# Linear attention's gate computed with its weights moving, its decay levels in three visits instead of four, and two changes of who issues DMAs

## The chip, the cores and the metric

The kernel runs on one core of a Trainium2 chip. TensorE (PE in the profile) multiplies, VectorE (DVE) and ScalarE (ACT) prepare operands and finish results, GpSimd (POOL) does little here, and SyncE (SP) issues nearly all DMAs. The metric is device time in microseconds of one launch, as the median of several runs.

## The reference, cut to what matters

Two layers on x (256 x 2048, fp32). Each layer projects x, runs three groups of heads, gates each with a SiLU path, projects back and normalizes:

```python
h = x @ w_in                                  # 2048 -> 6672 columns
a_q, a_k, a_v, a_z, b_q, b_k, b_v, b_z, b_lr, m_q, m_z = jnp.split(h, cuts, axis=-1)
y_a = chunk_band_attention(heads_a(a_q), heads_a(a_k), heads_a(a_v), rel_table)   # 8 heads of 128
log_g = log_sigmoid(b_lr @ gate_w + gate_b) / 16
o_b = gla_chunk_recurrence(b_q, b_k, b_v, log_g)     # linear attention, 4 heads, chunks of 64
y_b = o_b * rsqrt(mean(o_b**2) + 1e-6) * gla_norm_g
mk, mv = jnp.split(mem @ w_mem_kv, 2, axis=-1)
y_m = memory_attention(m_q, mk, mv)                  # 4 heads of 128
y = concat([y_a * silu(a_z), y_b * silu(b_z), y_m * silu(m_z)])
x = layer_norm(ALPHA * x + y @ w_out, ln_g, ln_b)
```

Within a chunk of 64 frames the linear attention (GLA) weighs frame j for frame i by exp(-|b_i - b_j|), where b is the running sum of the log gates, with one decay per key dimension.

## The kernel before

**Precision.** Every fp32 operand of the large products is split into a high part (`wh`, or `x[..., 0]`), rounded to the fp32r type, and a low part (`wl`, or `x[..., 1]`), which is the rest. A product is high times high, high times low and low times high. ScalarE casts the high part (line 261), VectorE subtracts to get the low part (line 268), each one or two loads ahead of TensorE.

**Two forms of a product.** Line numbers are those of the profile; every product is issued by the helper `mm` (line 86). In `stationary`, a 128x128 tile of the weights is loaded into the array and the activations move: for each 128 of the inner dimension two matmuls of 512 columns (high and low activations side by side, both against `wh`) and two of 256 (against `wl`). The result lies with features on the partitions. `ws_pieces` calls it for a group of 512 output features in two halves of four loads each, four units to a load, and hands each half to a `put` function. In `moving` the activations are loaded into the array and the weights move: three matmuls of 512 columns for each 128 tokens. The result lies with tokens on the partitions. `as_pieces` calls it for 512 features in eight loads, four units to a load. A load of either form is 512 KB, and a unit of either form streams 1536 columns: two matmuls of 512 and two of 256 in the one, three of 512 in the other.

**What sets the order.** TensorE and SyncE run in the order in which the program is written; the order of the other engines comes from a scheduler. `loads` is one list of all weight loads in the order of use. `take` hands out the next load and, ahead of it, issues later casts, subtractions and DMAs; a raw load goes to a ring of four buffers (`RAWS`), so a DMA on SP waits until the subtraction four loads back is done. The work of the heads is written as generators. `tick` is called once after each load (or each quarter product) and lets the generators whose time has come issue their next piece; `yield 3` means: go on three ticks later. A generator in `aside` (GLA, residual, norms) runs beside the heads in `waiting`, two heads at a time. `banks(n)` gives n of four PSUM banks, and yields until they are free. `finish` ticks until the named generators are done.

**GLA.** After the sums of the log gates, the attention inside a chunk is computed in levels (`LEVELS` 32 to 1, and -1 for the diagonal). For each level `distance` and `decayed` make decayed keys and queries on VectorE and ScalarE, each in a 128x512 buffer of the pool `sc` (eight buffers); TensorE then does 16 products of 64x64 (32 matmul records, since plain fp32 goes in two passes), and VectorE copies the part that belongs to the level into `pairs`. A turn of this on TensorE is a visit; there are four, of two, two, two and one levels, with two PSUM banks each (three in the last, which also makes the chunk states). After the visits come the products with the values and states, a norm (line 698) and four transposes per head parity (line 704), which write `yraw[0]` with features on the partitions.

**The gates.** Six groups follow the values: the second keys of the banded attention, the memory queries, then the gates b_z, a_z (two groups) and m_z, all as `ws_pieces`. `gate` adds the two halves of a result (`total`: line 497 on ScalarE, line 498 on VectorE), applies SiLU, waits with `finish` for its heads, multiplies `yraw` (line 1119) and, for b_z, splits it at once (`split_y`).

**Output stage and end.** The output projection works with seven products of blocks instead of eight (`out_unit`, letters B, K and T of the strings `OUT_B`, `OUT_A`; O is a plain `as_pieces`), so B and T loads are used for six matmuls and K and O loads for twelve. In the last layer `gain_rows` fetches the rows of ln_g and ln_b, broadcast to 128 partitions, as eight DMAs of 256 KB on POOL's queue, all in one place; `norm_residual` does the same for the layer before on SP's queue.

**Start.** `begin` issues on SP a quarter of the first activations (128 KB), the first weights (512 KB), the rest of these activations, and the second weights.

Of the kernel before, what the change touches and what calls it, by code (L numbers as in the profile page):

```python
# [16 lines left out]
P = 128  # L17
# [10 lines left out]
VISITS = ((-1, 0), (1, 2), (3, 4), (5,))  # L28
# [24 lines left out]
def hybrid_trunk_kernel(  # L53
# [71 lines left out]

    def banks(n):
        while len(free) < n:
            yield 1
        return [free.pop(0) for _ in range(n)]
# [11 lines left out]
    def plan():  # L141
        for l in range(L):
            def keys(p):
                g = w512[l, G_MK].rearrange("(h q) p n -> q p h n", h=2)
                return Load(g[p // 2, :, :, p % 2 * 512:p % 2 * 512 + 512], (2, 512))
# [46 lines left out]
            for g in (G_AK1, G_MQ, G_BZ, G_AZ0, G_AZ1, G_MZ):  # L192
                loads.extend(Load(w512[l, g, p], (4, 256)) for p in range(8))
# [143 lines left out]
    def begin():  # L337

        x, ws = loads[0], loads[1:3]
        xt = operand()  # L340
        x.quarter[0].append(xt)
        x.hi, x.lo = xt[:, :, 0], xt[:, :, 1]
        x.raw = res.rearrange("p t (s j n) -> p (t s) j n", s=2, j=4)[:, 0]
        for w in ws:
            w.raw = wp.tile([P, 2, 512], F32, name=nm("raw"), tag="raw")
            w.hi = wp.tile([P, 2, 512], F32R, name=nm("wh"), tag="wh", bufs=4)
            w.lo = wp.tile([P, 2, 512], F32R, name=nm("wl"), tag="wl", bufs=3)
        zero = zeros(dve, 256)
        whole = slice(None)
        first, second = slice(0, 256), slice(256, 512)  # L350
        for d, s in ((x, (whole, 0)), (ws[0], (whole,)), (x, (whole, slice(1, 4))), (ws[1], (whole,))):
            src = d.src if d is x else d.src.rearrange("p (k n) -> p k n", k=2)
            sp.dma_start(d.raw[s], src[s])
        parts = [(x, (whole, 0)), (ws[0], (whole, 0, first)), (ws[0], (whole, 0, second)), (ws[0], (whole, 1)), (x, (whole, 1)),
                 (x, (whole, 2)), (ws[1], (whole, 0)), (x, (whole, 3)), (ws[1], (whole, 1))]
        at["dma"] = 3
        for i in range(ZEROS):
            mm(ps[:, 2 + i % 2, :256], zero[:, :P], zero, True, True)
        for d, s in parts:
            cast = act.copy(d.hi[s], d.raw[s])  # L360
# [172 lines left out]
    def gla(gb, ng, gq, gk, asv, yraw):  # L533
# [38 lines left out]
        def distance(lev):  # L572
            s = LEVELS[lev]
            bm = b_.rearrange("p (g c) -> p g c", c=2 * s)
            dd = scratch([P, 512])
# [6 lines left out]
        def decayed(dd):  # L582
            kl = scratch([P, 512])
# [12 lines left out]
        yield 3  # L596

        kdT = yraw[:, 0:2].rearrange("p h (g c) -> p (h g) c", c=P)
        st = hd.tile([P, 3, 2, P], F32, name=nm("st"), tag="st")
        for v, levels in enumerate(VISITS):  # L600
# [8 lines left out]
            pb = yield from banks(3 if last else 2)  # L609
            for i, (lev, (kl, ql)) in enumerate(zip(levels, ready)):  # L610
                o = 256 if last else i * 256
                for t in range(2):
                    for b in range(2):
                        for half in range(2):
                            for par in range(2):
                                rs = slice(par * 64, par * 64 + 64)
                                c0 = b * T + t * P + half * CH
                                mm(ps[half * CH:(half + 1) * CH, pb[par], o + (t * 2 + b) * CH:o + (t * 2 + b + 1) * CH],
                                   kl[rs, c0:c0 + CH], ql[rs, c0:c0 + CH], True, True)
# [11 lines left out]
            for i, lev in enumerate(levels):  # L631
                o = 256 if last else i * 256
                for par in range(2):
                    pv = ps[:, pb[par], o:o + 256].rearrange("p (g c) -> p g c", c=CH)
# [30 lines left out]
        place = lambda par, half: slice((par ^ half) * CH, (par ^ half) * CH + CH)  # L665
        for g in range(4):
            t, b = g // 2, g % 2
            for par in range(2):
                for half in range(2):
                    hs = slice(half * CH, (half + 1) * CH)  # L670
                    mm(ps[place(par, half), bx[half], g * P:(g + 1) * P], pairs[par][hs, g],
                       asv[hs, t, 16 + (2 * b + par) * P:16 + (2 * b + par + 1) * P], True, True)
        for odd, even in ((1, 2), (3, None)):
            for b in range(2):
                for c in (odd, even):
                    if c is not None:
                        for par in range(2):
                            rs = slice(par * 64, par * 64 + 64)
                            g = (c // 2) * 2 + b
                            mm(ps[place(par, c % 2), by[par], g * P:(g + 1) * P],  # L680
                               qe[rs, b * T + c * CH:b * T + (c + 1) * CH], st[rs, c - 1, b], True, True)
        for half in range(2):
            for par in range(2):
                hs = place(par, half)
                act.copy(on[par][hs], ps[hs, bx[half]].rearrange("p (g c) -> p g c", c=P))
# [13 lines left out]
        yield 4  # L699
        for par in range(2):  # L700
# [4 lines left out]
            y = yraw.rearrange("p (b e) (t h c) -> p e h b t c", e=2, t=2, h=2)[:, par]  # L705
            o = ps[:, pt].rearrange("p (b t h c) -> p h b t c", b=2, t=2, h=2)
            for half in range(2):
                act.activation(y[:, half], o[:, half ^ par], AF.Copy, scale=ng[:, 0:1])
# [265 lines left out]
    for l in range(L):  # L974
# [102 lines left out]
        gens = [[gla(*gp, gq, gk, asv, yraw[0])]]  # L1077
# [35 lines left out]
        for i in range(4):  # L1113
            def gate(j, a, b):
                sz = gated()
                total(sz, a, b)
                act.activation(sz, sz, AF.Silu)  # L1117
                finish(gens[i])
                dve.tensor_tensor(yraw[i][:, j:j + 2], sz, yraw[i][:, j:j + 2], op=ALU.mult)  # L1119
                if i == 0:  # L1120
                    split_y(0, j)
                elif i == 3 and j == 2:
# [11 lines left out]
        if last:  # L1134
            rows = gain_rows(l)
# [133 lines left out]
```

## Time and profile before

| | |
|---|---|
| median of 3 runs | 913.99 us (912.38 to 914.93) |
| profiled execution, its own time | 913.39 us |
| its span, first to last instruction | 911.4 us (2.0 us lie around it) |
| granted TensorE clock | 0.999 |
| TensorE busy | 903.2 us of 911.4 |
| VectorE, ScalarE, GpSimd busy | 717.9, 551.8, 13.6 us |
| read from HBM | 193.16 MB |

A matmul's record is longer than the distance to the next one, because matmuls overlap; for the cost of a product the distance between starts is to be read, not the mean duration. In the timeline, a row merges neighbours of one kind (xcount), and an idle time in front is given in brackets with what ended it. In the windows, `DMA share` is the busy share of the 16 DMA engines.

### The profile page before, as it was taken

How to read it: one execution, taken by the hardware profiler on the slowest of the kernel's cores; microseconds unless marked ns; L12 is line 12 of the kernel's file. 1: busy time of each engine (PE TensorE's matmuls, PEld its weight loads, DVE VectorE, ACT ScalarE, POOL GpSimd, SP SyncE). 2: the span in 40 equal slices, each digit the busy share in tenths (PEclk: the TensorE clock that was granted, in tenths of full speed). 3: DMA queues.
4: the chain of work that ended last, by engine and by line, in shares of the span. 5: the costliest groups of instructions: out<-in, count | busy, mean ns of one | idle time of the engine just before them, and what ended most of it. 6: DMA issues, size and time to landing. Idle time of an engine off the chain costs nothing.

```text
span 911.4 us, 14553 instructions
## 1 busy us (share of the span) xinstructions
PE 903.2 (99%) x5491; PEld 795.3 (87%) x5491; DVE 717.9 (79%) x995; ACT 551.8 (61%) x809; POOL 13.6 (1%) x32
## 2 busy tenths in 40 slices
PE   9999999999999999999999999999999999999997
PEld 7889989998888888888888899999988888888885
DVE  5697688698766777799979767886886778778996
ACT  5675655576576675555559655556756667566540
POOL 1000000000000000000000000000000000100000
PEclk9999999999999999999999999999999999999999
DMA  8868786775445446876775787666754565776652
GB/s 298 293 195 288 262 266 206 236 253 180 160 145 161 159 161 187 289 272 223 236 243 167 206 291 254 223 196 186 218 177 134 178 192 185 273 277 232 229 190 93
DMA packets 64294, 196.21 MB, mean 215 GB/s; under 512 B 7008, under 2 KB 9568, under 8 KB 64224
## 3 DMA queue, kind: packets, MB, share of 16 engines
q1 hardware_dynamic: 63200, 193.08, 64.9%
q0 software_dynamic: 1024, 2.21, 0.8%
q8 instruction: 43, 0.70, 0.3%
q14 instruction: 27, 0.22, 0.1%
HBM read 193.16 MB, written 2.10 MB: 214 GB/s over the span
## 4 chain that ended last, share of the span: by engine, by line
PE 98%; DVE 1%; DMA 0%; ACT 0%; issue 0%; SPq 0%; DVEq 0%
PE ps L86 96%; PE ps L737 1%; DVE wl L268 0%; DMA raw<-w 0%; PE ps L833 0%; PE ps L775 0%; PE ps L704 0%; DVE sz L498 0%; DVE x L268 0%; ACT wh L261 0%; PE ps L606 0%; ACT res L877 0%; PE ps L541 0%; DVE term L260 0%; ACT wh L360 0%
## 5 line engine op out<-in xcount | busy, mean ns | idle before, releaser
L268 DVE TENSOR_TENSOR wl<-raw,wh 128x1024 fp32r<-128x1024 f32 (+1 forms) x313 | 364.8, 1169 | 118.5 <-PE ps L86 71.1
L261 ACT CAST wh<-raw 128x1024 fp32r<-128x1024 f32 (+1 forms) x313 | 313.9, 1008 | 233.4 <-PE ps L86 125.3
L86 PE MATMUL ps<-x,wh 128*128 128x512 f32 x1408 | 445.0, 397 | 0.0
L86 PEld LDWEIGHTS ps<-x,wl 128*128 128x128 f32 x1408 | 264.2, 188 | 63.2 <-DVE wl L268 1.0
L86 PE MATMUL ps<-x,wl 128*128 128x256 f32 x1408 | 277.5, 279 | 0.3 <-DVE wl L268 0.3
L86 PE MATMUL ps<-wh,x 128*128 128x512 f32 (+2 forms) x856 | 246.5, 369 | 0.9 <-ACT wh L360 0.9
L86 PEld LDWEIGHTS ps<-x,wh 128*128 128x128 f32 x1408 | 219.2, 189 | 1.6 <-issue 0.3
L86 PEld LDWEIGHTS ps<-wh,x 128*128 128x128 f32 x856 | 155.5, 188 | 19.7 <-ACT wh L360 1.1
L86 PE MATMUL ps<-wl,x 128*128 128x512 f32 (+2 forms) x428 | 157.8, 369 | 0.1
L86 PEld LDWEIGHTS ps<-wl,x 128*128 128x128 f32 x428 | 80.3, 188 | 10.5 <-DVE wl L268 0.6
L261 ACT CAST wh<-term 128x776 fp32r<-128x776 f32 (+1 forms) x39 | 36.0, 924 | 51.2 <-DVE term L260 43.3
L268 DVE TENSOR_TENSOR wl<-term,wh 128x776 fp32r<-128x776 f32 (+1 forms) x39 | 41.5, 1065 | 12.7 <-PE ps L86 12.0
L260 DVE TENSOR_TENSOR term<-term,term 128x776 f32<-128x776 f32 (+1 forms) x39 | 41.3, 1060 | 0.2 <-DMA term<-w 0.2
L86 PE MATMUL ps<-wh,s 128*128 128x512 f32 (+1 forms) x144 | 41.2, 367 | 0.0
L86 PEld LDWEIGHTS ps<-wh,s 128*128 128x128 f32 x144 | 25.8, 188 | 3.1
L86 PE MATMUL ps<-wl,s 128*128 128x512 f32 (+1 forms) x72 | 26.6, 370 | 0.3 <-DVE wl L268 0.3
L498 DVE SCALAR_TENSOR_TENSOR sz<-ps,sz 128x512 f32<-128x512 f32 x24 | 16.4, 687 | 5.0 <-ACT sz L497 4.1
L728 ACT ACTIVATE sc<-sc,mx 128x128 f32<-128x128 f32 (+1 forms) x32 | 14.2, 444 | 8.2 <-DVE mx L726 8.2
L86 PE MATMUL ps<-wh,sc 128*128 128x388 f32 x64 | 16.5, 338 | 0.0
L86 PEld LDWEIGHTS ps<-wl,s 128*128 128x128 f32 x72 | 13.5, 188 | 2.3 <-DVE wl L268 0.8
L1119 DVE TENSOR_TENSOR yr<-sz,yr 128x512 f32<-128x512 f32 x16 | 11.0, 687 | 4.6 <-ACT sz L1117 4.6
L1117 ACT ACTIVATE sz<-sz 128x512 f32<-128x512 f32 x16 | 10.1, 632 | 7.1 <-DVE sz L498 7.0
(222 smaller groups left out, 713.9 us busy)
## 6 DMA issues: line engine op xcount, KB each, us to landing
raw<-w SPq DMA_DIRECT2D x254, 512.0 KB, 4.3
raw<-w SPq DMA_DIRECT2D x64, 388.0 KB, 3.8
term<-w SPq DMA_DIRECT2D x24, 388.0 KB, 4.3
term<-w SPq DMA_DIRECT2D x15, 512.0 KB, 5.3
bias<-relw SPq DMA_DIRECT2D x16, 192.0 KB, 3.9
res<-xT SPq DMA_DIRECT2D x4, 512.0 KB, 6.9
res<-xn SPq DMA_DIRECT2D x4, 512.0 KB, 5.4
raw<-memT SPq DMA_DIRECT2D x4, 512.0 KB, 4.5
```

The source lines that it names most:

```text
L86: pe.matmul(o, l, r, start=start, stop=stop, skip_group_check=True)
L260: in_order(dve.tensor_tensor(d.raw, d.raw, d.plus, op=ALU.add))
L261: act.copy(d.hi, d.raw)
L268: in_order(dve.tensor_tensor(d.lo, d.raw, d.hi.bitcast(F32), op=ALU.subtract))
L498: dve.scalar_tensor_tensor(dst, a, scale, dst, op0=ALU.mult, op1=ALU.add)
L728: act.activation(s[:, own[t]], s[:, own[t]], AF.Exp, bias=mx[:, t:t + 1], accum_out=zs[:, t:t + 1])
L737: pe.transpose(ps[:, pt, i * P:(i + 1) * P], s[:, i * P:(i + 1) * P], ident)
L1117: act.activation(sz, sz, AF.Silu)
L1119: dve.tensor_tensor(yraw[i][:, j:j + 2], sz, yraw[i][:, j:j + 2], op=ALU.mult)
```

## The change

- `G_BZ`'s loads are cut as the memory keys' are (two runs of 512 instead of four of 256), and the group runs as `as_pieces` with its weights moving. Its `put`, `put_gate`, applies SiLU to the 128x1024 result straight from PSUM and hands it to GLA. `gla` multiplies its output (tokens on the partitions) by the gate before the four transposes, instead of `gate` doing it after them; the halves need no adding. `split_y(0, ...)` moves to the first half of the next gate.
- `VISITS` is three long, of three, three and one levels; the first two take four banks. A request for more than one bank now holds back requests for one (`wanted`). The third level's decayed keys and queries of the second visit go to `yraw[3]`.
- The copies after GLA's value products put each half of a chunk's rows in its place, so the last copy to `yraw[0]` is one per parity instead of two.
- `gain_rows` becomes a generator that issues one of its eight DMAs every two ticks, on SP's queue.
- The first quarter of the first activations is issued by ScalarE instead of SP.

```diff
-VISITS = ((-1, 0), (1, 2), (3, 4), (5,))
+VISITS = ((-1, 0, 1), (2, 3, 4), (5,))
...
     def banks(n):
-        while len(free) < n:
+        if n > 1:
+            wanted.append(n)
+        while len(free) < n or wanted and n == 1:
             yield 1
+        if n > 1:
+            wanted.remove(n)
         return [free.pop(0) for _ in range(n)]
...
             for g in (G_AK1, G_MQ, G_BZ, G_AZ0, G_AZ1, G_MZ):
-                loads.extend(Load(w512[l, g, p], (4, 256)) for p in range(8))
+                loads.extend(keys(p, g) if g == G_BZ else Load(w512[l, g, p], (4, 256)) for p in range(8))
...
-            sp.dma_start(d.raw[s], src[s])
+            (act if s == (whole, 0) else sp).dma_start(d.raw[s], src[s])
...
         ready = [(gkf, gqf), decayed(dd)]
         yield 3
+        ready.append(decayed(distance(1)))
+        yield 4
...
-            pb = yield from banks(3 if last else 2)
+            pb = yield from banks(3 if last else 4)
...
-                for lev in VISITS[v + 1]:
-                    dd = distance(lev)
+                for n, lev in enumerate(VISITS[v + 1]):
+                    mine, other = (extra[:, h * 2:h * 2 + 2].rearrange("p h t -> p (h t)") if n == 2 else None for h in range(2))
+                    dd = distance(lev, mine)
                     yield 1
-                    ready.append(decayed(dd))
+                    ready.append(decayed(dd, other))
                     yield 1
-                yield 1
+                yield 3
...
             dve.tensor_tensor(on[par], on[par], rr[:, par * 4:par * 4 + 4].unsqueeze(2).to_broadcast([P, 4, P]), op=ALU.mult)
-        yield 4
+        gate.append(None)
+        while len(gate) < 2:
+            yield 1
+        z = gate[1].rearrange("p t (b e d) -> p e (t b) d", e=2, d=P)
+        for par in range(2):
+            dve.tensor_tensor(on[par], on[par], z[:, par], op=ALU.mult)
+        yield 2
...
-    def gain_rows(l):
-        rows = []
+    def gain_rows(l, rows):
         for n in range(4):
-            g, b = scratch([P, 512]), scratch([P, 512])
-            pool.dma_start(g, ln_g[l:l + 1, columns(n)].to_broadcast([P, 512]))
-            pool.dma_start(b, ln_b[l:l + 1, columns(n)].to_broadcast([P, 512]))
-            rows.append((g, b))
-        return rows
+            pair_ = []
+            for a in (ln_g, ln_b):
+                pair_.append(scratch([P, 512]))
+                sp.dma_start(pair_[-1], a[l:l + 1, columns(n)].to_broadcast([P, 512]))
+                if a is ln_b:
+                    rows.append(pair_)
+                yield 2
...
+        def put_gate(acc):
+            while not z_gate:
+                tick()
+            z = hd.tile([P, 2, 512], F32, name=nm("z"), tag="qb")
+            act.activation(z, acc, AF.Silu)
+            z_gate.append(z)
+
+        run(as_pieces(xq[l], 512, put_gate, True))
+        for i in range(1, 4):
             def gate(j, a, b):
...
+                if i == 1 and j == 0:
+                    finish(gens[0])
+                    split_y(0, 0)
+                    split_y(0, 2)
                 finish(gens[i])
                 dve.tensor_tensor(yraw[i][:, j:j + 2], sz, yraw[i][:, j:j + 2], op=ALU.mult)
-                if i == 0:
-                    split_y(0, j)
```

How the order of instructions changes, at three places. In the rows, a buffer's number stands behind its name; `sc` are buffers of the pool of eight, `x` the four quarters of the activations, `qk` heads' queries and keys, `asv` the values.

First, TensorE in layer 0, at GLA's first visit, which before lay among the value loads (388 columns):

```order
L86 MATMUL ps<-wh_1870,x_474 128x388 x2
L86 MATMUL ps<-wl_1917,x_474 128x388
L606 MATMUL ps<-ident,sc_1819 128x128 x4
L86 MATMUL ps<-gq_506,gk_507 64x64 x16
L86 MATMUL ps<-sc_1824,sc_1888 64x64 x16
L86 MATMUL ps<-wh_1915,x_526 128x388 x2
L86 MATMUL ps<-wl_1942,x_526 128x388
```

and after the change:

```order
L86 MATMUL ps<-wh_1983,x_565 128x388 x2
L86 MATMUL ps<-wl_2013,x_565 128x388
L617 MATMUL ps<-ident,sc_1819 128x128 x4
L86 MATMUL ps<-gq_506,gk_507 64x64 x16
L86 MATMUL ps<-sc_1824,sc_1888 64x64 x16
L86 MATMUL ps<-sc_1976,sc_1980 64x64 x16
L86 MATMUL ps<-x_434,wh_2011 128x512 x2
L86 MATMUL ps<-x_434,wl_2031 128x256 x2
```

The first visit now has three levels and stands some loads later, between the last value load and the first load of the second keys.

Second, TensorE in layer 0 at GLA's transposes. Before, they stand beside products of a banded head in the memory queries' group, a load ahead of the gate's:

```order
L704 MATMUL ps<-ident,sc_2546 128x128 x4
L704 MATMUL ps<-ident,sc_2547 128x128 x4
L86 MATMUL ps<-sc_2685,asv_522 128x256
L86 MATMUL ps<-sc_2685,asv_522 128x128
L86 MATMUL ps<-sc_2690,asv_522 128x256
L86 MATMUL ps<-sc_2690,asv_522 128x128
L86 MATMUL ps<-x_565,wh_2660 128x512 x2
L86 MATMUL ps<-x_565,wl_2694 128x256 x2
```

and after the change:

```order
L86 MATMUL ps<-x_474,wh_2911 128x512 x2
L86 MATMUL ps<-x_474,wl_2937 128x256 x2
L721 MATMUL ps<-ident,sc_2675 128x128 x4
L721 MATMUL ps<-ident,sc_2676 128x128 x4
L86 MATMUL ps<-x_526,wh_2935 128x512 x2
L86 MATMUL ps<-x_526,wl_2959 128x256 x2
```

The transposes now stand behind the gate's eight loads, two loads (32 matmuls) and one memory head's first products into the next group. On ScalarE, the gate's SiLU (`z`) stands among the weight casts like this:

```order
L268 CAST wh_2935<-raw_2869 128x1024
L761 COPY yr_1679<-ps 128x256 x2
L268 CAST wh_2957<-raw_2897 128x1024
L1134 ACT_TABLE_LOAD
L1134 ACTIVATE z_2953<-ps 128x1024
L268 CAST wh_3005<-raw_2915 128x1024
L780 ACT_TABLE_LOAD
```

The cast behind `z` waits with it for the last matmul of the gate.

Third, SyncE in layer 1's output stage, before (`term` and `raw` are buffers of weights):

```order
L231 DMA term_8001<-w 128x1024
L238 DMA raw_8057<-w 128x1024
L238 DMA raw_8106<-w 128x1024
L238 DMA raw_8118<-w 128x1024
L238 DMA raw_8131<-w 128x1024
L238 DMA raw_8149<-w 128x1024
L238 DMA raw_8161<-w 128x1024
```

and after the change:

```order
L238 DMA term_7917<-w 128x1024
L245 DMA raw_7973<-w 128x1024
L245 DMA raw_8006<-w 128x1024
L821 DMA sc_8014<-ln_g 128x512
L245 DMA raw_8020<-w 128x1024
L245 DMA raw_8033<-w 128x1024
L821 DMA sc_8047<-ln_b 128x512
L245 DMA raw_8053<-w 128x1024
L245 DMA raw_8065<-w 128x1024
L821 DMA sc_8079<-ln_g 128x512
```

One row DMA now stands ahead of every second weight DMA, eight times in all.

More of the change, by code (lines that the diff above doesn't have):

```diff
@@ L531, in gla_inputs, with gla @@
         return gb, ng
-    def gla(gb, ng, gq, gk, asv, yraw):
+    def gla(gb, ng, gq, gk, asv, yraw, gate, extra):
         gqf = gq.rearrange("p b t -> p (b t)")
@@ L570, in gla, with distance @@
         act.activation(eb, b_, AF.Exp, scale=1.0 / 16)
-        def distance(lev):
+        def distance(lev, dd=None):
             s = LEVELS[lev]
             bm = b_.rearrange("p (g c) -> p g c", c=2 * s)
-            dd = scratch([P, 512])
+            if dd is None:
+                dd = scratch([P, 512])
             dve.tensor_tensor(dd.rearrange("p (g c) -> p g c", c=2 * s), bm,
@@ L664, in gla @@
         by = bx[2:]
-        place = lambda par, half: slice((par ^ half) * CH, (par ^ half) * CH + CH)
+        rows = lambda half: slice(half * CH, (half + 1) * CH)
         for g in range(4):
@@ L669, in gla @@
                 for half in range(2):
-                    hs = slice(half * CH, (half + 1) * CH)
-                    mm(ps[place(par, half), bx[half], g * P:(g + 1) * P], pairs[par][hs, g],
+                    hs = rows(half)
+                    mm(ps[rows(par ^ half), bx[half], g * P:(g + 1) * P], pairs[par][hs, g],
                        asv[hs, t, 16 + (2 * b + par) * P:16 + (2 * b + par + 1) * P], True, True)
@@ L704, in gla @@
                     pe.transpose(ps[:, pt, b * T + t * P:b * T + (t + 1) * P], on[par][:, t * 2 + b], ident)
[L705 to L708, printed above, removed]
+            y = yraw.rearrange("p (b e) t -> p e b t", e=2)[:, par]
+            act.activation(y, ps[:, pt].rearrange("p (b t) -> p b t", b=2), AF.Copy, scale=ng[:, 0:1])
             release(pt)
@@ L1134, in hybrid_trunk_kernel @@
         if last:
-            rows = gain_rows(l)
+            rows = []
+            beside([gain_rows(l, rows)])
             gbrow = per.tile([2, 1024], F32, name="gbrow", tag="yr0")
```

33 lines of the change are left out of this document (17 added, 16 removed).

## The prediction

> **What bounds the kernel now.** I read the page first, then the chain, then TensorE's own waits.
>
> ```profile
> span 911.4 us, 14553 instructions
> PE 903.2 (99%) x5491; PEld 795.3 (87%) x5491; DVE 717.9 (79%) x995; ACT 551.8 (61%) x809; POOL 13.6 (1%) x32
> PE 98%; DVE 1%; DMA 0%; ACT 0%; issue 0%; SPq 0%; DVEq 0%
> ```
>
> TensorE is busy for 903.2 of 911.4 us, and the chain that ended last runs through it for 98%. So an instruction taken from VectorE or ScalarE is worth nothing by itself, and a DMA is worth something only where TensorE stands still for it. What is left: the distance between starts of matmuls, the few places where TensorE is held up, and the start. The holdups are short, and a busy engine hides them, since a matmul's record is longer than its distance to the next. In the timeline they are gaps between starts; the three largest behind the start:
>
> ```profile
> 58.41 0.63 PE L86 MATMUL ps<-x,wh 128*128 128x512 f32 x2
> 59.31 0.50 PE L86 MATMUL ps<-x,wl 128*128 128x256 f32 x2 [0.26 <-DVE wl L268]
> ...
> 379.72 0.63 PE L86 MATMUL ps<-wh,s 128*128 128x512 f32 x2
> 380.67 0.50 PE L86 MATMUL ps<-wl,s 128*128 128x512 f32 x1 [0.31 <-DVE wl L268]
> ...
> 395.36 0.61 PE L86 MATMUL ps<-wh,x 128*128 128x512 f32 x2
> 396.12 0.50 PE L86 MATMUL ps<-wl,x 128*128 128x512 f32 x1
> ```
>
> Two matmuls of 512 take about 0.46 us from start to start; here they take 0.90, 0.95 and 0.76. That is 0.44 + 0.49 + 0.30 = 1.2 us lost to late low parts, at a layer's first own products and in layer 0's output stage. The change reorders nothing there.
>
> **The change part by part.** *The gate with weights moving.* The first two rows are the first and last of 15 units in the b_z group of layer 0 (stationary form), then the next instruction; the last two span seven units of the moving form.
>
> ```profile
> 272.38 0.63 PE L86 MATMUL ps<-x,wh 128*128 128x512 f32 x2
> ...
> 282.60 0.39 PE L86 MATMUL ps<-x,wl 128*128 128x256 f32 x2
> 282.83 0.38 PE L737 MATMUL ps<-ident,sc 128*128 128x128 f32 x2
> ...
> 442.18 0.62 PE L86 MATMUL ps<-wh,x 128*128 128x512 f32 x2
> ...
> 446.94 0.39 PE L86 MATMUL ps<-wh,x 128*128 128x512 f32 x1
> ```
>
> Stationary: (282.83 - 272.38) / 15 = 0.697 us a unit. Moving: (446.94 - 442.18) / 7 = 0.680 us. Both stream 1536 columns; the difference of 0.017 us is what four matmuls cost more than three. The gate has 8 loads of 4 units, 32 in a layer and 64 in both: 64 x 0.017 = 1.09 us less, all on TensorE's path. I take the whole, since both forms run here without a wait.
>
> The Trainium skill speaks against this size: "TensorE: Matmul & The Clock Gate", section "Wait — 56ns, not 53.3ns?", has warm matmuls start N/2.4 GHz plus about 2.5 ns apart, so one matmul less in each of 64 units would be worth an estimated 0.16 us. By it the sum would be 0.9 us smaller. The trace does not agree: a third of 0.680 is 0.227 us for 512 columns, 11 ns more than by that rule.
>
> *Three visits instead of four.* Every level keeps its 32 small matmuls; what goes is one change from the large products to small ones and back. The price comes from the visit of two levels, and from the first visit, where the levels follow each other.
>
> ```profile
> 197.46 0.69 PE L86 MATMUL ps<-gq,gk 64*64 64x64 f32 x32
> 197.98 0.65 PE L86 MATMUL ps<-sc,sc 64*64 64x64 f32 x32
> 198.55 0.62 PE L86 MATMUL ps<-wh,x 128*128 128x388 f32 x2
> ...
> 228.40 0.63 PE L86 MATMUL ps<-x,wh 128*128 128x512 f32 x2
> 228.87 0.39 PE L86 MATMUL ps<-x,wl 128*128 128x256 f32 x2
> 229.19 1.16 PE L86 MATMUL ps<-sc,sc 64*64 64x64 f32 x64
> 230.28 0.73 PE L86 MATMUL ps<-x,wh 128*128 128x512 f32 x2
> 230.84 0.40 PE L86 MATMUL ps<-x,wl 128*128 128x256 f32 x2
> ```
>
> From 228.40 to 230.84 are 2.44 us; without the visit they would be two pairs of 512 (0.47 each) and one of 256 (0.23), 1.17 us, so the visit cost 1.27. A level inside costs at least 0.45 and at most 0.52 (197.46 to 197.98, which holds some of the way in). Two levels are 0.90 to 1.04, and the change back and forth 0.23 to 0.37. I take 0.30 a layer, 0.6 us in all (bounds 0.46 to 0.74). That the first visit moves behind the value loads changes nothing, since it is inserted in the same way there.
>
> What could be late instead: the three levels wait for four banks, and heads that want one wait too. A head that waits costs nothing as long as its gate does not come first. In the written order of the changed kernel the last memory head ends at the same row as before, 176 large matmuls ahead of the output stage, so that cover holds. If it did not, `finish` would tick without large products in between, and TensorE would see the whole latency of a head's steps.
>
> *The gate's tail.* The adding of halves goes (four pairs of operations on ScalarE and VectorE), off the path, so nothing. New: the transposes wait for SiLU and for the multiplication, which wait for the gate's last matmul. The nearest rows are a copy of 128x1024 from PSUM, a table load and a multiplication of 128x512:
>
> ```profile
> L501 ACT CAST mv<-ps 128x1024 fp32r<-128x1024 f32 x2 | 2.0, 1009 | 0.0
> L1117 ACT ACT_TABLE_LOAD x6 | 7.7, 1283 | 0.1
> L698 DVE TENSOR_TENSOR sc<-sc,rr 128x512 f32<-128x512 f32 x4 | 2.6, 688 | 0.1
> ```
>
> 1.28 + 1.01 + 2 x 0.69 = 3.7 us. Between the gate's end and the transposes stand two loads of large products, 8 x 0.697 = 5.6 us, and a memory head's products. Queued behind `z` on ScalarE is a cast for a load some three ahead, and behind the multiplication on VectorE a subtraction. So I cost it at nothing, with 1.9 us to spare; a cast and a subtraction of weights, both at the wrong moment, could use that up, and TensorE would then stand for what is left over.
>
> *Loads in runs of 2 KB instead of 4 KB* for the gate: 16 loads, in a stage whose DMA share is small (first row below). Nothing.
>
> *The norm's rows on SP's queue.* The 2 MB leave POOL, where they moved before the output stage, and go among its weight loads; SP pays an issue each.
>
> ```profile
> 778.52 0.38 SPq L849 DMA_DIRECT2D sc<-ln_g  x1
> sc<-ln_g POOLq DMA_DIRECT2D x4, 256.0 KB, 6.2
> 268.00:290.00 22.00, 22.00 (x131) 19.38 (x131) 16.01 (x26) 15.50 (x25) 0.00 (x0) 1.00 0.51 161
> 374.00:380.00 6.00, 6.00 (x28) 4.90 (x27) 2.44 (x3) 2.07 (x4) 0.00 (x0) 1.00 1.03 414
> 820.00:840.00 20.00, 20.00 (x90) 16.56 (x89) 17.49 (x18) 12.28 (x14) 0.00 (x0) 1.00 0.67 226
> ...
> 845.00:850.00 5.00, 5.00 (x24) 4.14 (x23) 4.66 (x5) 2.11 (x2) 0.00 (x0) 1.00 0.96 346
> 840.00:860.00 20.00, 20.00 (x90) 16.57 (x89) 18.34 (x18) 10.26 (x11) 0.00 (x0) 1.00 0.66 231
> ```
>
> At the 414 GB/s that the engines reach when full, 256 KB take 0.63 us; with 0.38 us of issue a row can delay the weights behind it by 1.0 us, eight rows by 8.1. The share in 820 to 860 is 0.67, and 2.1 MB over 40 us add 0.13, so 0.80: not full. The holdup at 380 came only after six full microseconds (1.03). The cost lies between 0 and 8.1; I take 0, since the nearest rows (0.67) lie far from the one where TensorE stood still. That POOL's burst goes gains nothing, as TensorE did not wait there.
>
> *The first activations by ScalarE.*
>
> ```profile
> 0.74 0.38 SPq L353 DMA_DIRECT2D res<-memT  x1
> 1.18 0.42 SPq L353 DMA_DIRECT2D raw<-w  x1
> ...
> 3.10 0.40 ACT L360 CAST x<-res 128x256 fp32r<-128x256 f32 x1 [1.08 <-DMA res<-memT]
> 5.12 1.23 ACT L360 CAST wh<-raw 128x256 fp32r<-128x256 f32 x3 [1.62 <-DMA raw<-w]
> ...
> 5.57 0.50 PE L86 MATMUL ps<-wh,x 128*128 128x256 f32 x2 [0.86 <-ACT wh L360]
> ```
>
> TensorE's first product waits for the cast of the weights at 5.12, and their DMA was issued at 1.18, behind the activations'. Now it can go at 0.74: 0.44 us earlier at most, and nothing at least, if the two transfers share the engines and the weights land when they did. Activations were ready two microseconds early, so a table load behind an issue of 0.38 us on ScalarE is covered. I take 0.35, nearer the upper end, since the DMAs behind move up too.
>
> *The sum.* 1.09 + 0.6 + 0.35 = 2.0 us less. The profiled execution took 913.39 us (911.4 of span and 2.0 around it), so 911.4; the median of the runs shown stands 0.6 higher, at 913.99, so 912.0 us, 0.22% less than before.
>
> **Rivals.** *The gate gains nothing.* The 0.017 us of a unit may belong to the stage (its loads into the array, its banks) and not to the fourth matmul; then the gate's stage keeps its 0.697. For it speaks that I compare two stages; against, that the moving rows lie in several stages alike. 912.0 + 1.1 = 913.1 us, no change. The Trainium skill's 2.5 ns, from the page named above, would come out near here, at about 912.9. Chance 0.14.
>
> *The holdups go too.* If fewer operations on VectorE and ScalarE, or the earlier start, let the late low parts be in time, 1.2 us go on top: 910.8. Against it: the work around the three places is the same, and the one at 380 comes from full DMA engines. Chance 0.14.
>
> *The rows starve the weights* (the other side). One mechanism, in layer 1's output stage: eight rows ahead of weight DMAs, four raw buffers, each delay passed on to TensorE. All of it gives 912.0 + 8.1 = 920.1. It makes the kernel slower by over 0.3% once more than 4.8 of the 8.1 us arrive; with 2.1 the whole gain is eaten up. For it: the share of 0.96 at 845 to 850; against it: TensorE was busy through those five microseconds too. Chance 0.10.
>
> **How the numbers follow.** The forecast holds 0.62, with 911.1 to 912.9 from the bounds of its terms. Differences under 0.3% (2.7 us) are about what a measurement of this kernel cannot tell from none; faster means below 911.25. That has 0.07 of the forecast's chance, all of the holdups' 0.14 and a little of the rest: 0.23. Slower (above 916.7) is most of the starved rows: 0.08. The rest is 0.69. The range goes down to 910.3 (the holdups gone, and half a microsecond of scatter) and up to 914.3 (the gate without gain and a microsecond of starved rows).
>
> **What the profile after would show.** Right: units of 0.680 in the b_z group with rows `ps<-wh,x` and `ps<-wl,x`; three visits a layer, two of them with 96 small matmuls; first product near 5.2; the three gaps as before; no new gap ahead of the output's transposes of GLA, and none in layer 1's output stage. Wrong: a first product still at 5.57; a gap with VectorE's multiplication named in front of the GLA transposes; gaps behind low parts between 815 and 860, with a DMA share near 1.

## The result, and the profile after

The changed kernel takes 926.45 us (median of 4 runs, 926.07 to 926.79); the kernel before, on the same chip, took 913.18. The ratio is 1.0143, with a 95% interval of 1.0124 to 1.0162: 13 us slower, where 912.0 us was forecast. The page and TensorE's own waits (what it waited for, us in all, times, longest), to be held against the page of before:

```profile
span 924.2 us, 14426 instructions
PE 906.5 (98%) x5427; PEld 794.4 (86%) x5427; DVE 715.1 (77%) x991; ACT 549.2 (59%) x799; POOL 8.9 (1%) x24
```

```profile
PE ps L752 <- DVE sc L747: 4.7, 5, 1.3
PE ps L86 <- DVE pairs L649: 1.5, 2, 0.8
PE ps L86 <- ACT sc L696: 1.4, 4, 0.4
PE ps L86 <- DVE wl L275: 1.4, 3, 0.7
...
PE ps L86 <- ACT wh L367: 1.1, 1, 1.1
PE ps L86 <- ACT yr L618: 1.1, 2, 0.5
```

VectorE and ScalarE have less to do than before (715.1 for 717.9 us, 549.2 for 551.8), and TensorE waits for them all the same. Four of these rows are new kinds of wait: head transposes (L752) for the head's softmax on VectorE (L747), head scores for the masked copies of a visit (L649), head products for copies out of the value products' banks (L696), and, inside a visit, small products for the copy of the transposed keys (L618).

The largest stands where the first head transposes of layer 0 come. The timeline of TensorE there, in the changed kernel:

```profile
199.80 0.34 PE L86 MATMUL ps<-wl,x 128*128 128x388 f32 x1
200.83 0.70 PE L752 MATMUL ps<-ident,sc 128*128 128x128 f32 x3 [0.69 <-DVE sc L747]
202.83 0.95 PE L752 MATMUL ps<-ident,sc 128*128 128x128 f32 x3 [1.30 <-DVE sc L747]
203.43 0.99 PE L86 MATMUL ps<-wh,x 128*128 128x388 f32 x2
...
206.22 0.52 PE L86 MATMUL ps<-wh,x 128*128 128x388 f32 x2
```

From 199.80 to 203.43 are 3.63 us for what takes 0.76 where nothing is late (198.69 to 199.45 in the run with the third level held, below), and the three units up to 206.22 take 2.79 us instead of 1.67. That is 4.0 us. The same place in layer 1 costs 4.1 (wait on a low part 1.0, the transposes 3.1), so 8.1 of the 13 us lie here. The windows show what VectorE does meanwhile; columns are window, length, busy time and count of TensorE, its weight loads, VectorE, ScalarE, GpSimd, then the granted clock, DMA share and GB/s. Changed kernel first, then one window of the kernel before:

```profile
200.00:203.00 3.00, 1.01 (x5) 0.52 (x4) 3.00 (x8) 1.08 (x2) 0.00 (x0) 0.91 0.86 283
203.00:206.00 3.00, 3.00 (x11) 2.92 (x12) 0.72 (x2) 2.24 (x5) 0.00 (x0) 0.52 0.86 322
```

```profile
200.00:203.00 3.00, 3.00 (x21) 2.96 (x20) 2.43 (x5) 2.17 (x4) 0.00 (x0) 1.00 0.60 218
```

TensorE does 1.01 us of work in three, VectorE is full, and the clock granted next is 0.52. VectorE's timeline shows what came ahead of the softmax (L747):

```profile
187.70 0.69 DVE L584 TENSOR_TENSOR yr<-qb 128x512 f32<-128x512 f32 x1
...
193.89 0.69 DVE L593 TENSOR_TENSOR yr<-gk,yr 128x512 f32<-128x512 f32 x1
...
196.08 0.68 DVE L594 TENSOR_TENSOR yr<-gq,yr 128x512 f32<-128x512 f32 x1
...
200.49 0.54 DVE L747 TENSOR_SCALAR sc<-sc,zs 128x128 f32<-128x128 f32 x2
```

The rows that write `yr` are the third level of the *second* visit. In the program they come after the first visit (213 us); their inputs are ready early and their output has a tile of its own, so the scheduler put them up to 25 us ahead, before the softmax on which TensorE waits next. The three rows are 2.1 us of work; the softmax ends 5.6 us later than in the kernel before (203.04 for 197.43), as the rows around them are ordered differently too. How much of it belongs to the early work, the run with the third level held shows.

The other new waits, all beside visits and value products:

```profile
213.33 0.74 PE L86 MATMUL ps<-sc,sc 64*64 64x64 f32 x34
214.60 0.69 PE L86 MATMUL ps<-sc,sc 64*64 64x64 f32 x30 [0.53 <-ACT yr L618]
...
246.20 1.58 PE L86 MATMUL ps<-qk,qk 128*128 128x128 f32 x8 [0.77 <-DVE pairs L649]
...
269.22 0.92 PE L86 MATMUL ps<-sc,asv 128*128 128x256 f32 x4 [0.45 <-ACT sc L696]
270.42 0.81 PE L86 MATMUL ps<-sc,asv 128*128 128x256 f32 x3 [0.28 <-ACT sc L696]
```

In distances between starts they cost 0.74, 0.84 and 1.1 us, and the same again in layer 1: 5.4 us. Each time a bank is handed on in the program as soon as its last reader is *issued*; TensorE's next small step takes it and waits until that reader is *done*. The rest: start and a new gap at 74 us add 1.0, layer 1's later heads 0.6; the gate, the saved visit and two gaps of layer 0's output stage that are gone take off 2.5. Together 12.6, of the 12.7 us between the two profiled executions (926.07 and 913.39).

### The profile page after: what moved, and what is told of

Read it like the earlier page. It is cut to its first block, busy times and chain, and to the rows that moved or that the text cites. A ratio compares the mean times of both kernels' runs of the same rounds, so it can differ in the third digit from the quotient of the medians.

```text
span 924.2 us, 14426 instructions
## 1 busy us (share of the span) xinstructions
PE 906.5 (98%) x5427; PEld 794.4 (86%) x5427; DVE 715.1 (77%) x991; ACT 549.2 (59%) x799; POOL 8.9 (1%) x24
## 5 line engine op out<-in xcount | busy, mean ns | idle before, releaser
L86 PE MATMUL ps<-x,wh 128*128 128x512 f32 x1280 | 404.3, 397 | 0.0
L86 PEld LDWEIGHTS ps<-x,wl 128*128 128x128 f32 x1280 | 240.5, 188 | 57.7 <-DVE wl L275 1.5
L86 PE MATMUL ps<-wh,x 128*128 128x512 f32 (+2 forms) x984 | 287.8, 374 | 1.1 <-ACT wh L367 1.1
L86 PE MATMUL ps<-x,wl 128*128 128x256 f32 x1280 | 252.5, 279 | 0.6 <-DVE wl L275 0.6
L86 PEld LDWEIGHTS ps<-wh,x 128*128 128x128 f32 x984 | 180.2, 189 | 24.3 <-ACT wh L367 1.3
L86 PEld LDWEIGHTS ps<-x,wh 128*128 128x128 f32 x1280 | 199.6, 189 | 1.6 <-issue 0.3
L86 PE MATMUL ps<-wl,x 128*128 128x512 f32 (+2 forms) x492 | 183.4, 373 | 0.8 <-DVE wl L275 0.7
L86 PEld LDWEIGHTS ps<-wl,x 128*128 128x128 f32 x492 | 92.7, 188 | 14.1 <-DVE wl L275 1.6
L868 DVE TENSOR_TENSOR res<-res,sc 128x512 f32<-128x512 f32 x16 | 10.3, 688 | 5.7 <-DMA sc<-ln_g 5.2
L86 PE MATMUL ps<-w,x 128*128 128x512 f32 (+1 forms) x72 | 14.3, 357 | 0.0
```

Source lines behind the costliest of these rows:

```text
L86: pe.matmul(o, l, r, start=start, stop=stop, skip_group_check=True)
L868: dve.tensor_tensor(r, r, row, op=op)
```

## The experiments

**The parts alone.** Each kernel is the one before with one part of the change.

Gate alone (all of the diff but `VISITS`, `banks`, the visits' loops, the DMA of the start and `gain_rows`):

> The kernel before with the gate's part of the change alone: moving weights in the gate, the product with silu ahead of the transposes, its tail before the second output group. Theory (the visits and the start cost the time, the gate does not): 64 units of 0.697 us become 64 of 0.680 us, so 1.1 us faster than before, 0.999, and no new idle time on TensorE around the gate. Rival (the gate's new place costs part of the 12.7 us): slower by 1 us or more, 1.001 or above, with a wait of TensorE on VectorE's product or on the output group's first piece.

Measured: 914.5 us, ratio 1.0008 (0.9996 to 1.0020). Neither theory: no gain, and none of the waits that the rival names (the interval leaves out the 1.1 us of the theory). The chain and TensorE's timeline of this run, in layer 1's output stage:

```profile
791.51 9.16 DMA raw<-w
...
802.96 1.23 DVE wl L271
```

```profile
804.23 0.50 PE L86 MATMUL ps<-x,wl 128*128 128x256 f32 x2 [1.30 <-DVE wl L271]
```

512 KB of weights were under way for 9.16 us while POOL's eight rows of the norm were moving, and TensorE lost 1.5 us here and 0.4 at 788. The kernel before has the same burst and does not wait between 780 and 810 us. That this kernel reaches the stage in another rhythm and meets the burst differently is inferred from that, not shown.

Visits alone (`VISITS`, `wanted` in `banks`, four banks, `extra`, the two longer yields):

> The kernel before with the visits' part alone: three later visits instead of four, so 11 calls to two levels with four PSUM banks, and a third level's work computed ahead into a spare tile. Theory (the visits are where the time went): 11 to 13 us slower than before, 1.012 to 1.014: in each layer about 4 us at the head transposes that wait for VectorE's head softmax, 0.7 us in the middle of the visit that takes the banks of the key transposes, 0.8 us after the second visit and 1.1 us after the value products. Rival (the head transposes wait because of the gate's tail, and only the bank waits belong to the visits): 4 to 6 us slower, 1.005 to 1.006, with the head softmax ahead of the transposes in time. Rival on record (the visits save their changes): 0.6 us faster.

Measured: 928.15 us, 1.0162 (1.0148 to 1.0175), so 14.9 us slower, more than the 11 to 13 of the theory. The waits of the changed kernel stand at the same places, and at a later head of layer 1 (741 to 744 us) the transposes wait 1.4 us where the changed kernel waits 0.3. The visits alone carry the loss, and the gate's tail has no part in it.

Start alone, and norm rows alone:

> The kernel before with the first 128 KB of activations issued by ScalarE's queue instead of SP's, nothing else. Theory (the two queues share the transfer time, so the small one lands later): first product at about 5.9 instead of 5.57 us, and with a later wait of up to 0.6 us near 74 us the kernel is 0.3 to 1.0 us slower, 1.0003 to 1.001. Rival (the later gap near 74 us is the weight stream's of another part of the change): 0.3 to 0.4 us slower. Rival on record: 0.35 us faster, 0.9996.

> The kernel before with the norm's gain and bias rows issued one at a time by SP's queue between the weights, nothing else. Theory (nobody waits for the rows, and the weights behind them have slack): the same time within 0.3 us, 1.000. Rival (the rows push weight loads back so that casts and with them TensorE wait): 0.6 us (the new wait at 74 us) up to 8.1 us slower, with the gaps on weight tiles.

Measured: start 913.5 us, 0.9999 (0.9990 to 1.0008); rows 912.71 us, 0.9997 (0.9989 to 1.0006). Neither can be told from nothing. The rows' rival falls. Of the start, the time cannot say whether 0.4 us are lost or won, but the timeline of the changed kernel can:

```profile
0.74 0.40 ACTq L360 DMA_DIRECT2D res<-memT  x1
0.74 0.39 SPq L360 DMA_DIRECT2D raw<-w  x1
...
5.17 0.40 ACT L367 CAST x<-res 128x256 fp32r<-128x256 f32 x1 [2.71 <-DMA res<-memT]
5.48 1.23 ACT L367 CAST wh<-raw 128x256 fp32r<-128x256 f32 x3
5.93 0.54 PE L86 MATMUL ps<-wh,x 128*128 128x256 f32 x2 [1.11 <-ACT wh L367]
```

The activations, cast at 3.10 before, are now cast at 5.17, as soon as they land, and the cast of the weights stands behind theirs. The weights landed 4.2 us after their issue at 0.74, at 4.9; before it was 3.9 us after 1.18, at 5.1. Issued 0.44 us earlier, they gained 0.1 to 0.2. The first product starts at 5.91 to 6.06 us in the seven profiles with this start, and at 5.43 to 6.14 (median 5.61) in the nine with SP's.

**The third level held.** Changed kernel with

```diff
+            held = behind if dd is not None else lambda instruction: None
-            dve.tensor_tensor(dd.rearrange(...), bm, ..., op=ALU.subtract)
+            held(dve.tensor_tensor(dd.rearrange(...), bm, ..., op=ALU.subtract))
```

where `behind` keeps an instruction after all that is written ahead of it on its engine.

> The changed kernel with one edit: the subtraction that begins a third level is held on VectorE in the order in which it is written, so the third level's work can't be pulled ahead of the head softmax. Theory (VectorE reaches the head softmax late because the third level's three passes of 0.69 us, with room of their own in a spare tile, stand ahead of it): the head transposes' waits of 4.7 us in the chain shrink below 1 us, the stretch after them keeps its full clock, and the kernel is 5 to 8 us faster than the changed one: 918 to 921 us, 1.006 to 1.009 of the kernel before. Rival (the small steps have lost the first visit that stood ahead of them as cover): VectorE is free earlier, but the transposes still wait, and the time stays at 925 to 926.

Measured: 917.75 us, 1.0054 (1.0036 to 1.0072), 8.7 us less than the changed kernel and just below the range of the theory. VectorE's softmax rows and TensorE's transposes:

```profile
196.24 1.01 DVE L748 TENSOR_SCALAR sc<-sc,zs 128x128 f32<-128x128 f32 x4
```

```profile
198.69 0.34 PE L86 MATMUL ps<-wl,x 128*128 128x388 f32 x1
198.87 0.82 PE L753 MATMUL ps<-ident,sc 128*128 128x128 f32 x6
199.45 0.60 PE L86 MATMUL ps<-wh,x 128*128 128x388 f32 x2
```

The softmax ends at 197.25 instead of 203, the transposes follow the products directly. The early work is shown to be the cause of the 8 us.

**Only the cover taken away.** Kernel before, with `yield 7` for `yield 3` ahead of the first visit.

> The kernel before with one edit: the first visit comes four steps later, so it stands behind the first head transposes, as in the changed kernel, with the levels and banks of before. Theory (the transposes wait for VectorE's extra early work, not for the cover that the visit gave): the first transposes wait below 0.5 us in each layer, and the time is within 1 us of before. Rival (the visit's 1.73 us ahead of the transposes was their cover): the transposes wait 1 to 2 us in each layer, with a slower clock behind them, and the time is 2 to 6 us above before, 1.002 to 1.007.

Measured: 914.42 us, 1.0012 (1.0003 to 1.0021). The visit is behind the transposes, and they do not wait:

```profile
200.07 0.34 PE L86 MATMUL ps<-wl,x 128*128 128x388 f32 x1
200.25 0.82 PE L737 MATMUL ps<-ident,sc 128*128 128x128 f32 x6
```

The 0.9 us come from another place: the moved last visit is followed by head transposes that take its bank, and TensorE waits for VectorE's copies 0.46 us in each layer. So the lost cover alone is not the cause; whether the visit, left in its old place, would have hidden part of a softmax that is late, no run shows. A bank taken too early costs here too.

**Gate and rows.** Changed kernel with the visits and the start of before.

> The changed kernel with the four visits of before and the first activations by SP again: what is left is the gate with moving weights and the norm rows one by one by SP's queue. Theory (in the gate-only kernel's profile the waits of 0.4 and 1.5 us at 788 and 803 us come from 512 KB of weights that share the transfers with POOL's eight norm rows; issued one by one between the weights the rows no longer meet them): 1 to 2 us faster than before, 0.998 to 0.999, with no wait above 0.3 us between 780 and 810 us. Rival (the gate moves the weights' stream as a whole, whoever issues the rows): 1.000 to 1.002, with the same waits.

Measured: 913.22 us, 0.9993 (0.9984 to 1.0002). No wait is left between 780 and 810. The weights' DMAs in 776 to 806 us (count, size, median us to landing), gate alone and then gate with rows:

```profile
raw<-w SPq DMA_DIRECT2D x9, 512.0 KB, 8.2
```

```profile
raw<-w SPq DMA_DIRECT2D x11, 512.0 KB, 3.7
```

So the theory on the burst holds by these rows, which come from one profile of each kernel. The times show 0.6 us less than before, with an interval from 1.5 less to 0.2 more: a gain near 1 us is neither shown nor excluded, one of 2 us is excluded. (The first product of the profiled execution came at 6.14 us, 0.57 later than before.)

**Banks handed on later.** First all at once, with generous delays: `yield 2` ahead of `release(pt)` of the keys, `yield 3` ahead of `release(*pb)` (and `yield 1` for 3 behind each visit), `yield 2` ahead of `release(*bx)`, the third level held, SP's start.

> The changed kernel with three visits, but the third level held as written, the key transposes' bank, the visits' banks and the value products' banks handed on 2, 3 and 2 steps later than their last reader is issued, and the first activations by SP. Theory (the loss is early work on VectorE and banks handed on before they are read, not the number of visits): all waits at the head transposes, the visits, the scores and the value products go, and the time is 911 to 914 us, 0.998 to 1.001 of before. Rival (three visits with four banks starve the heads, so any delay comes back as a head that its gate waits for): 917 to 922 us, with waits at new places.

Measured: 935.08 us, 1.0236 (1.0223 to 1.0249), slower than the changed kernel and beyond the rival's range. The named waits are gone, and others take their place: head products for a copy on ScalarE, 5.0 us in each layer, and 6.1 us in all for VectorE at other heads. ScalarE and TensorE at the largest, in the timeline:

```profile
293.19 1.28 ACT L514 ACT_TABLE_LOAD   x1
...
294.81 1.28 ACT L1138 ACT_TABLE_LOAD   x1
...
296.10 1.02 ACT L1138 ACTIVATE z<-ps 128x1024 f32<-128x1024 f32 x1
297.02 0.86 ACT L758 COPY sc<-ps 128x384 f32<-128x384 f32 x2
...
297.55 0.79 PE L86 MATMUL ps<-sc,asv 128*128 128x256 f32 x1 [4.96 <-ACT sc L758]
```

GLA's end has slid next to a head's transposes; eight squares, two table loads, two casts of weights and `z` stand on ScalarE ahead of the head's copy (L758), and TensorE waits 5.0 us. A delay is a move, and what stands at the new place counts.

Then one at a time, one step each, on the kernel with the third level held (917.75 us); where a visit's banks are delayed, the step behind each visit is shortened by one (`yield 2` for 3):

> The kernel with the third level held, and the key transposes' bank handed on one step later, so that the first visit doesn't take it right behind them. Theory (each bank that is handed on as soon as its last reader is issued makes TensorE wait for that reader): the wait for ScalarE's copy in the middle of the first visit (0.73 us in each layer) goes and nothing else, 1.5 us faster than with the third level held: about 916.3. Rival (the visit moves a step and another small step meets a reader instead): 917 to 920, with a wait at a new place of the same layer.

> The kernel with the third level held, and a visit's banks handed on one step later. Theory (as in the run beside it): the head's scores no longer wait for VectorE's masked copies after the second visit (0.98 us in each layer, of which 0.14 are an ordinary change of shape), 1.7 us faster than with the third level held: about 916. Rival (the third visit and the value products move a step, next to another head's small steps): 917 to 920, with a wait at a new place.

> The kernel with the third level held, and the value products' four banks handed on one step later. Theory: the head's products no longer wait for ScalarE's copies out of those banks (0.7 and 0.45 us in each layer), 2.3 us faster than with the third level held: about 915.5. Rival (ScalarE's four copies and eight squares stand ahead of the head's own copy in its queue, so the head waits for ScalarE whichever bank it is given): 917 to 918, the wait on another row.

> The changed kernel with the third level held and all three hand-ons one step later (one, not the two and three of the kernel before it, where ScalarE's work on the value products came ahead of a head's copy). Theory: the 5.5 us of the three waits go, 911.5 to 913 us, 0.998 to 1.000 of before, so that the visits are worth the change that they save, some 0.6 us, and no more. Rival (small steps pushed together meet VectorE or ScalarE again): 915 us or more, with waits above 0.5 us in the chain.

Measured: keys' bank 913.9 us (1.0010, 1.0000 to 1.0019); visits' banks 918.12 (1.0052, 1.0037 to 1.0066); value products' banks 915.18 (1.0019, 1.0009 to 1.0030); all three 915.84 (1.0026, 1.0015 to 1.0038). TensorE's timeline where each still waits, in the order keys, visits, all three:

```profile
214.54 1.58 PE L86 MATMUL ps<-qk,qk 128*128 128x128 f32 x8 [0.83 <-DVE pairs L651]
```

```profile
258.54 0.55 PE L754 MATMUL ps<-ident,sc 128*128 128x128 f32 x3 [0.57 <-ACT sc L756]
```

```profile
261.82 0.55 PE L756 MATMUL ps<-ident,sc 128*128 128x128 f32 x3 [0.57 <-ACT sc L758]
```

The value products' delay does what the theory said (2.6 us for 2.3). The keys' delay gains 3.9 for 1.5: by moving what follows it also parts the value products from the head behind them, and leaves the wait of a head's scores, now after the first visit. The visits' delay gains nothing, as its rival says: its own wait goes, the last visit lands ahead of a head's transposes, and the value products' wait grows. All three together reach 915.84 us and not the 911.5 to 913 of the theory. Each wait is a pair of neighbours, so delays do not add up.

**Small steps spaced.** Last, TensorE's order was chosen so that at least 12 plain products stand between a visit or value product and the next step that takes one of its banks. Both kernels hold the third level, delay the keys' and the value products' banks by one step, and start with SP; in the first the visits begin one step later (`yield 5` for 4), in the second one earlier (`yield 3`) with one more step behind each visit (`yield 4` for 3).

> Three visits with the third level held, the key transposes' and the value products' banks one step later, the first visit one step later, and the first activations by SP: in TensorE's order at least 12 plain products then stand between each visit or value product and the next small step that takes one of its banks. Theory (the loss was all in VectorE's early work and in banks taken before they are read): no wait above 0.5 us in the middle of a layer, and 911.5 to 912.7 us, 0.9985 to 0.9995 of before, which is the gate's 1.1 us and at most the visits' 0.6 us. Rival (three visits put more on VectorE and ScalarE at once than a head leaves free, wherever they stand): 913.5 to 916, with waits at the head transposes.

> The same mends with another spacing: the first visit one step earlier than in the changed kernel and one step more behind each visit. Theory: as in the run beside it, 911.5 to 912.7 us; the first visit comes sooner after its levels, so its wait, if any, is on VectorE's product of the second level. Rival (the early first visit meets VectorE's full stretch at 188 to 200 us): 913.5 to 916, with waits at the first visit or the first head transposes of each layer.

Measured: 912.49 us (0.9990, 0.9979 to 1.0001) and 911.22 us (0.9974, 0.9965 to 0.9983). The first cannot be told from the kernel before; the second beats it by 1.6 to 3.2 us and lies just below the range of its theory. The second's waits on TensorE, complete, and a visit of three levels in its timeline:

```profile
PE ps L86 <- DVE eps L991: 1.2, 1, 1.2
PE ps L86 <- ACT wh L367: 0.9, 1, 0.9
PE ps L86 <- ACT row L892: 0.3, 1, 0.3
```

```profile
207.74 0.33 PE L86 MATMUL ps<-wl,x 128*128 128x388 f32 x1
208.00 0.69 PE L86 MATMUL ps<-gq,gk 64*64 64x64 f32 x32
208.52 1.11 PE L86 MATMUL ps<-sc,sc 64*64 64x64 f32 x64
209.56 0.72 PE L86 MATMUL ps<-x,wh 128*128 128x512 f32 x2
210.12 0.40 PE L86 MATMUL ps<-x,wl 128*128 128x256 f32 x2
```

Only start and end are left. Three visits do not cost what the changed kernel loses wherever they stand; this kernel keeps the four banks and the rule of `wanted` in `banks` too, so neither costs anything by itself that shows here. The 2.4 us (interval 1.6 to 3.2) hold the 1.7 that the prediction added up for gate and visits, but do not show it by themselves: the gaps at 59, 380 and 396 us (1.2 together) are not in this profile either, though other kernels' profiles show one or two of them, and the first of the two kernels, with the same gate and visits, gained 0.8.

## Why the prediction was wrong, point by point

- **The gate: the price of a unit right.** In the changed kernel's b_z group eleven units run from the first of these rows to the second, 7.48 / 11 = 0.680 us each, as foretold:

```profile
281.47 0.62 PE L86 MATMUL ps<-wh,x 128*128 128x512 f32 x2
...
288.95 0.82 PE L752 MATMUL ps<-ident,sc 128*128 128x128 f32 x6
```

  So the rival of a gate without gain falls. But the gain does not arrive by itself: alone, the gate met the norm rows' burst (914.5 us), and with the rows issued one by one the time was 0.6 us less, not clear of noise. "That POOL's burst goes gains nothing" held for the rhythm of before only.
- **The visits: the step that failed.** Forecast was a gain of 0.6 us; alone they cost 14.9. Their own price on TensorE was right: from 207.74 to 210.12 are 2.38 us, 0.65 without the visit, so 1.73 for three levels, against 1.27 for two. Two visits of 1.73 for three of 1.27 save 0.35 us a layer; 0.30 was taken. But "what goes is one change from the large products to small ones and back" priced TensorE alone. It left out that the third level's room lets VectorE's work run early (8.1 us in the changed kernel's timeline), and that four banks leave none over: whoever takes a bank next waits for a reader (5.4 us). "A head that waits costs nothing as long as its gate does not come first" is true of a head that waits for a bank in the program, and not of TensorE when it has been given the bank and waits for its last reader. I looked for lateness at the last head, and the loss lay at the first and at every bank. "That the first visit moves behind the value loads changes nothing" was off by 0.9 us (0.3 to 1.9), since a later visit meets another neighbour.
- **"An instruction taken from VectorE or ScalarE is worth nothing by itself"** was read from the shares of the span, and it hid the other direction: work moved ahead, in a stretch where VectorE is full, cost 8 us.
- **The gate's tail: right** in the changed kernel, no wait stands ahead of GLA's transposes. With GLA's end moved, the table loads and `z` behind it did hold TensorE up.
- **The norm's rows: right** for the kernel before: alone they change nothing that shows (between 1.0 us less and 0.5 more), and there is no gap in 815 to 860. So the rival of starved weights falls.
- **The start: wrong sign in the timelines**, though too small for the times to show. First product at 5.93, not near 5.2. The step "if the two transfers share the engines and the weights land when they did" was the lower end, at a gain of nothing; the activations, called two microseconds early, became the neck, which the bounds of 0 to 0.44 us did not provide for. The Trainium skill, "DMA: Bandwidth & Descriptors", section "Issuing engines are not separate DMA queues", says that transfers of several engines interleave on the same DMA engines; the 5.17 above agrees.
- **The rivals:** the holdups of layer 0's output stage did largely go (none at 380 and 396, one of 0.2 at 402), lost in the rest. No rival put the slower side at the visits, so the range of 910.3 to 914.3 had no room for it.

## What to carry to other kernels

Before pricing a merged step by the bound engine's own time, list for every small step behind it which engine must have read its bank or finished its input, and how many plain products stand between. Give early-ready work a buffer of its own only together with a place in the order, else a scheduler puts it ahead of what the bound engine waits for next. A delay mends one pair of neighbours and makes another; look at the whole order, then run it.

## What the runs showed of the hardware

Gaps of 2.0 us in layer 0 (0.69 and 1.30) were followed by three microseconds at a granted clock of 0.52, which added 1.1 us to the wait itself; 2.4 us of gaps at the same place in layer 1 (1.11 and 1.30) were not, the products of 388 columns behind them keeping their 0.53 us a unit at a granted clock of 1.00. The visits alone show the same in the same two places. The slow stretch lasted 3.4 us at 0.50 in both kernels (202.5 to 205.9 in the changed one), and in the kernel with generous delays each gap of 5.0 us came with 6.8 us at 0.50, twice as long (from 295.5 us in layer 0). The Trainium skill, "TensorE: Matmul & The Clock Gate", section "What's actually happening", has the activity judged in windows that run free of the kernel, which would allow both; no run here shows the windows themselves, or how little work in one is enough to lower the clock.
